# Storing two result tiles of a batched matmul in three transfers each: 112, 8 and 8 partitions over two DMA queues

## The chip, the cores and the metric

The kernel runs on one core of a Trainium2 chip. The metric is device time in microseconds (us), the median of several executions. A core has a matrix engine (TensorE, "PE" in the profile, with its weight loads as "PEld"), VectorE ("DVE"), ScalarE ("ACT"), GpSimd ("POOL") and SyncE ("SP"). They work on an on-chip memory of 128 partitions and on the matrix engine's accumulators. Transfers between this memory and the large outer memory ("dram") run on sixteen DMA engines; an instruction on GpSimd, SyncE or ScalarE issues such a transfer into that engine's own queue, and the transfer tells of its end by a semaphore.

## The reference

```python
def setup_inputs():
    return {
        "a": np.random.randn(1024, 64, 64).astype(np.float32),
        "b": np.random.randn(1024, 64, 64).astype(np.float32),
    }

def reference(a, b):
    return np.matmul(a, b).astype(np.float32)
```

1024 independent products of 64 x 64 matrices. Each of `a`, `b` and the result has 16.8 MB, and each is moved once.

## The kernel before

The batch is cut into 16 tiles `t` of 64 matrices for `b` and the result, and 8 double tiles `s` of 128 matrices for `a`. A tile of `b` or of the result is 1 MB.

**Loads.** `load_a` (L70) brings a double tile in four parts: three by GpSimd's queue, which convert to bf16 on the way (L74), and one by SyncE's queue in fp32 (L78). The first double tile is loaded by SyncE and ScalarE (L91). `load_b` (L94) brings a tile of `b` by SyncE's queue for even `t` and by ScalarE's for odd `t` (L97), three tiles ahead.

**Compute.** Each `a` is transposed, by VectorE (L128) for double tiles 1 to 3 and by the matrix engine (L138, copied out at L141) for the others. `spread` (L146) lays the transposed blocks into a block-diagonal operand (L154, L164), `cast` (L169) turns `b` into bf16: VectorE at L173, and for the last tile ScalarE (L180) and VectorE (L178) by quarters. `multiply` (L187) runs 64 matmuls per tile (L218), and `evacuate` (L200) copies the accumulators into the result tile `o_sb` (L206), mostly on ScalarE; for odd tiles from 7 on, half of the second half's copies go to VectorE.

**Stores.** `o_sb` holds, for each of 128 partitions, eight pieces (`gh`) of 1 KB, 8 KB in all. In the outer memory each such piece is one run of 1 KB:

```python
    o_v = out.rearrange("(t gh x) (mo w) n -> t (x mo) gh (w n)", gh=8, x=8, w=4)
```

`multiply` does not store: it leaves functions in `held[t]`, which `store(t)` (L183) calls later. `HOLD = 2` (L38), so the main loop (L258) calls `store(t - 1)` at the end of its turn for `t` (L286). For tiles 0 to 13 there is one function, which calls `put(0, 8)` (L194): one transfer of all 128 partitions, 1 MB, issued by GpSimd (L195; `store_queue`, L65). Tile 14 goes in two halves by SyncE, tile 15 in quarters by ScalarE and SyncE in turns. Result tiles come from a pool of eight buffers.

**Order.** The program's order is each engine's order: an engine issues its transfers and runs its instructions as written, and waits where an operand isn't ready. SyncE's list from tile 11 on is: the load of `b`'s tile 14, then the stores of tiles 14 and 15. ScalarE issues the load of `b`'s tile 15 in the loop's turn 12. GpSimd's last two instructions are the stores of tiles 12 and 13.

Of the kernel before, what the change touches and what calls it, by code (L numbers as in the profile page):

```python
# [13 lines left out]
def kernel(  # L14
# [14 lines left out]
    nc = tc.nc  # L29
# [7 lines left out]
    N_BD = 2  # L37
    HOLD = 2  # L38
    ON_DVE = (1, 2, 3)

    a_v = a.rearrange("(s g h) (mp v) k -> s h g mp (v k)", h=4, g=32, v=16)
    b_v = b.rearrange("(t g h) (kp u) n -> t (h kp) g (u n)", h=4, g=16, u=2)
    o_v = out.rearrange("(t gh x) (mo w) n -> t (x mo) gh (w n)", gh=8, x=8, w=4)
# [19 lines left out]
    held = {}  # L63

    def store_queue(t, lo):  # L65
        if t < n_t - 2:
            return nc.gpsimd
        return nc.scalar if t == n_t - 1 and lo % 4 == 0 else nc.sync

    def load_a(s):  # L70

        a_sb = a_pool.tile([128, 3, 16, 64], bf16, name="a_sb")
        for h in range(3):
            nc.gpsimd.dma_start(  # L74
                out=a_sb[:, h, :, :].rearrange("p v k -> p (v k)"), in_=a_v[s, h], single_packet=True
            )
        a_raw = a_pool.tile([128, 16, 64], fp32, name="a_raw")
        nc.sync.dma_start(out=a_raw[:].rearrange("p v k -> p (v k)"), in_=a_v[s, 3])  # L78
        a_tiles[s] = a_sb, a_raw
# [53 lines left out]
    def transpose(s, j):  # L133
        a_cols = abf_tiles[s][:].rearrange("p v h k -> p v (h k)").bitcast(fp32)
        for wl in range(2):
            at_ps = t_psum.tile([128, 4, 128], fp32, name="at_ps")
            for vo in range(4):
                nc.tensor.transpose(  # L138
                    at_ps[:, vo, :], a_cols[:, 4 * vo + 2 * j + wl, :], identity[:]
                )  # L140
            nc.scalar.copy(  # L141
                at_tiles[s][:, :, 2 * j + wl, :, :],
                at_ps[:].rearrange("p vo (g mp) -> p g mp vo", mp=4),
            )

    def spread(t):  # L146
        bd = bd_tiles[t % N_BD]
        at_sb = at_tiles[t // 2]
        for h in range(4):
            rows = slice(32 * h, 32 * h + 32)  # L150
            if t // 2 in ON_DVE:
                for i in range(2):
# [34 lines left out]
    def multiply(t):  # L187
        at_bd = bd_tiles[t % N_BD][:].rearrange("p g (j wl) h mp vo -> p j g (wl h mp vo)", j=2)
        at_bd = at_bd.bitcast(bf16).rearrange("p j g (c u) -> p j g c u", u=2)
        b_bf = bbf_tiles.pop(t)  # L190
        last = t == n_t - 1
        o_sb = o_pool.tile([128, 8, 2, 2, 64], fp32, name="o_sb")

        def put(lo, n):  # L194
            store_queue(t, lo).dma_start(  # L195
                out=o_v[t, :, lo : lo + n, :],
                in_=o_sb[:, lo : lo + n].rearrange("p gh j wl n -> p (gh j wl n)"),
            )

        def evacuate(o_ps, gh, n, copies):  # L200

            for par in range(2):
                for wl in range(2):
                    src = o_ps[64 * wl : 64 * wl + 64, :, par, :, :]
                    dst = o_sb[64 * par : 64 * par + 64, gh : gh + n, :, wl, :]
                    copies[2 * par + wl](dst, src)  # L206

        for half in range(2):
            if not last:
                o_ps = o_psum.tile([128, 4, 2, 2, 64], fp32, name="o_ps")  # L210
            for g8 in range(8):
                if last and g8 % 4 == 0:
                    o_ps = t_psum.tile([128, 2, 2, 2, 64], fp32, name="at_ps")
                g = 8 * half + g8
                gl = (g8 % 4 if last else g8) // 2
                for j in range(2):
                    for u in range(2):
                        nc.tensor.matmul(  # L218
                            o_ps[:, gl, g % 2, j, :],
                            at_bd[:, j, g, :, u],  # L220
                            b_bf[:, g, 64 * u : 64 * u + 64],
                            start=(u == 0),
                            stop=(u == 1),
                        )
                if last and g8 % 4 == 3:
                    copy = nc.scalar.copy if g8 == 3 else nc.vector.tensor_copy
                    evacuate(o_ps, g // 4 * 2, 2, [copy] * 4)
            if not last:
                copies = [nc.scalar.copy] * 4
                if half and t % 2 and t > 2 * max(ON_DVE):  # L230
                    copies[2:] = [nc.vector.tensor_copy] * 2
                evacuate(o_ps, 4 * half, 4, copies)
        if last:
            held[t] = [lambda q=q: put(2 * q, 2) for q in range(4)]
        else:
            whole = t < n_t - 2
            held[t] = [lambda q=q: put(q, 8 if whole else 4) for q in ([0] if whole else [0, 4])]

    with tc.manual_schedule():
        load_first_a()  # L240
# [17 lines left out]
        for t in range(n_t):  # L258
            s, half = t // 2, t % 2
            if t + 1 < n_t:  # L260
                spread(t + 1)
                cast(t + 1)
            if t + B_AHEAD < n_t:
                load_b(t + B_AHEAD)
            if half == 0 and 0 < s < n_s - 1 - A_AHEAD:
                load_a(s + 1 + A_AHEAD)
            if half == 0 and 0 < s < n_s - 1 and s + 1 not in ON_DVE:
                transpose(s + 1, 1)
            multiply(t)
            if t == 0:  # L270
                transpose_dve(1, 0)
                transpose_dve(1, 1)
                a_tiles.pop(1)
                load_a(A_AHEAD)
                load_a(A_AHEAD + 1)
            if t and s + 2 in ON_DVE and (half or s):
                for part in [0, 1] if t == 1 else [half]:
                    transpose_dve(s + 2, part)
                if half:
                    a_tiles.pop(s + 2)  # L280
            elif half == 0 and 0 < s and s + 2 < n_s:
                regroup(s + 2)
            elif half == 1 and s + 2 < n_s:
                transpose(s + 2, 0)
            if t >= HOLD - 1:
                store(t - HOLD + 1)  # L286
# [32 lines left out]
```

## Time and profile before

| what | value |
|---|---|
| median of 3 runs | 133.72 us (133.55 to 133.87) |
| the profiled execution | 133.61 us, of which span 131.8 us |
| busy share of the span: PE, PEld, DVE, ACT, POOL | 45%, 43%, 77%, 67%, 24% |
| outer memory read, written | 33.55 MB, 16.78 MB; 382 GB/s over the span |
| stores by GpSimd (L195) | 14 of 1024 KB, median 22.7 us from issue to landing |
| stores by SyncE | 2 of 512 KB (5.5 us), 2 of 256 KB (5.2 us) |
| stores by ScalarE | 2 of 256 KB (4.7 us) |
| issue of the stores of tiles 12 and 13 on GpSimd | at 109.93 us (0.90 us) and 115.72 us (1.35 us) |

The span runs from the first to the last instruction of the program; what lies around it (1.8 us here) is start and end of the execution. "Landing" is the last completion of a transfer. The store of tile 12 takes from 109.93 to 122.9 us to land, that of tile 13 from 115.72 to 125.6 us.

### The profile page before, as it was taken

The page shows a single profiled execution, that of the slowest core. Times are in us where ns is not written, and L with a number is a line of the kernel's source. Part 1 is how long each engine was busy: PE and PEld are TensorE (multiplying, and loading weights), DVE is VectorE, ACT ScalarE, POOL GpSimd, SP SyncE. Part 2 cuts the span into 40 slices and gives each one's busy share as a digit, 9 for nine tenths or more (in the row PEclk, how much of TensorE's full clock was granted, in tenths as well). Part 3 has the DMA queues.
Part 4 walks back from the last instruction along what each step waited for, and adds up shares of the span by engine and source line. Part 5 has one row for each costly group of instructions (what it writes and reads, how often), then busy time and mean ns, then how long its engine had stood idle before and what let it go on. Part 6 is the DMA issues. An engine that isn't in the chain of part 4 may idle for free.

```text
span 131.8 us, 2750 instructions
## 1 busy us (share of the span) xinstructions
PE 59.6 (45%) x1104; PEld 56.7 (43%) x1104; DVE 101.8 (77%) x144; ACT 88.1 (67%) x158; POOL 31.9 (24%) x43
## 2 busy tenths in 40 slices
PE   0006405730550640908662883299369619465000
PEld 0006305730550630908552872298368618464000
DVE  5930399529999984999999998699999997898300
ACT  2125414999495096492999989469969996549920
POOL 8991000340054000618031204300420302040000
PEclk9999975798568555595999599558968975579855
DMA  3999999999999999999999999999999999999993
GB/s 68 372 334 313 306 313 280 280 311 321 327 299 400 362 306 297 393 393 400 321 285 357 403 395 362 308 299 385 395 391 393 390 390 397 399 395 406 390 383 136
DMA packets 19020, 44.99 MB, mean 341 GB/s; under 512 B 1088, under 2 KB 3136, under 8 KB 19008
## 3 DMA queue, kind: packets, MB, share of 16 engines
q0 software_dynamic: 6832, 20.19, 50.6%
q1 hardware_dynamic: 7120, 14.68, 30.7%
q10 hardware_dynamic: 5056, 9.96, 20.1%
q8 instruction: 8, 0.13, 0.4%
q14 instruction: 4, 0.03, 0.1%
HBM read 33.55 MB, written 16.78 MB: 382 GB/s over the span
## 4 chain that ended last, share of the span: by engine, by line
DMA 53%; ACT 15%; DVE 14%; PE 6%; issue 5%; SPq 2%; ACTq 0%; DVEq 0%
DMA b_sb<-in_b_dram 53%; ACT o_sb L206 12%; PE o_ps L218 6%; DVE at_bd L164 4%; DVE b_bf L173 4%; DVE at_bd L154 2%; ACT b_bf L173 1%; DVE at_sb L128 1%; DVE o_sb L206 1%; DVE a_bf L109 1%; SPq L91 1%; ACT a_bf L126 1%; SPq L97 1%; ACT b_bf L180 1%; DVE a_bf L112 0%
## 5 line engine op out<-in xcount | busy, mean ns | idle before, releaser
L206 ACT COPY o_sb<-o_ps 64x512 f32<-64x512 f32 x112 | 65.0, 581 | 17.9 <-PE o_ps L218 13.5
L218 PEld LDWEIGHTS <-at_bd 128*128 128x128 bf16 x1024 | 45.2, 117 | 52.6 <-DVE b_bf L173 40.5
L218 PE MATMUL o_ps<-b_bf,at_bd 128*128 128x64 bf16 x960 | 45.6, 223 | 48.7 <-DVE b_bf L173 35.0
L164 DVE COPY at_bd<-at_sb 32x1024 f32<-32x1024 f32 x40 | 29.6, 739 | 6.6 <-ACT at_sb L141 5.6
L195 POOL DMA_DIRECT2D out_dram<-o_sb x14 | 15.4, 1103 | 46.1 <-ACT at_sb L141 20.6
L154 DVE COPY at_bd<-at_sb 32x512 f32<-32x512 f32 x48 | 22.0, 457 | 1.1
L74 POOL DMA_DIRECT2D a_sb<-in_a_dram x21 | 12.4, 606 | 38.5 <-DVE at_sb L128 33.2
L173 DVE CAST b_bf<-b_sb 128x2048 bf16<-128x2048 f32 x14 | 17.2, 1227 | 5.2 <-DMA b_sb<-in_b_dram 4.9
L138 PE MATMUL at_ps<-identity,a_bf 128*128 128x128 f32 x80 | 12.9, 329 | 11.0 <-ACT a_bf L106 11.0
L138 PEld LDWEIGHTS at_ps<-identity,a_bf 128*128 128x128 f32 x80 | 11.7, 176 | 11.0 <-issue 11.0
L141 ACT COPY at_sb<-at_ps 128x512 f32<-128x512 f32 x20 | 10.8, 591 | 2.7 <-PE at_ps L138 2.0
L128 DVE STREAM_TRANSPOSE at_sb<-a_sb 128x512 f32<-128x512 f32 x9 | 8.9, 1065 | 0.0
L128 DVE STREAM_TRANSPOSE at_sb<-a_bf 128x512 f32<-128x512 f32 x3 | 3.1, 1049 | 4.0 <-ACT a_bf L126 4.0
L206 DVE COPY o_sb<-o_ps 64x512 f32<-64x512 f32 x8 | 5.5, 690 | 0.2
L106 ACT CAST a_bf<-o_sb 128x1024 bf16<-128x1024 f32 x2 | 2.1, 1045 | 5.0 <-DMA o_sb<-in_a_dram 5.0
L173 ACT CAST b_bf<-b_sb 128x2048 bf16<-128x2048 f32 x1 | 1.9, 1897 | 4.0 <-DMA b_sb<-in_b_dram 4.0
L126 ACT CAST a_bf<-a_raw 128x1024 bf16<-128x1024 f32 x3 | 3.1, 1046 | 1.7 <-DMA a_raw<-in_a_dram 1.7
L109 DVE COPY a_bf<-a_sb 128x3072 bf16<-128x3072 bf16 x4 | 4.2, 1045 | 0.0
L106 DVE CAST a_bf<-o_sb 128x1024 bf16<-128x1024 f32 x2 | 2.8, 1383 | 1.8 <-DMA o_sb<-in_a_dram 1.8
L246 DVE MEMSET at_bd<- 128x4096 f32 x1 | 3.5, 3472 | 0.8 <-issue 0.8
L206 DVE COPY o_sb<-at_ps 64x256 f32<-64x256 f32 x8 | 3.4, 422 | 0.5 <-PE at_ps L218 0.4
L180 ACT CAST b_bf<-b_sb 128x512 bf16<-128x512 f32 x2 | 1.1, 616 | 3.5 <-DMA b_sb<-in_b_dram 3.5
(16 smaller groups left out, 15.4 us busy)
## 6 DMA issues: line engine op xcount, KB each, us to landing
out_dram<-o_sb POOLq DMA_DIRECT2D x14, 1024.0 KB, 22.7
a_sb<-in_a_dram POOLq DMA_DIRECT2D x21, 256.0 KB, 15.9
a_raw<-in_a_dram SPq DMA_DIRECT2D x7, 512.0 KB, 17.3
o_sb<-in_a_dram SPq DMA_DIRECT2D x2, 512.0 KB, 5.9
o_sb<-in_a_dram ACTq DMA_DIRECT2D x2, 512.0 KB, 7.0
out_dram<-o_sb SPq DMA_DIRECT2D x2, 512.0 KB, 5.5
out_dram<-o_sb SPq DMA_DIRECT2D x2, 256.0 KB, 5.2
out_dram<-o_sb ACTq DMA_DIRECT2D x2, 256.0 KB, 4.7
```

The lines of the kernel that those rows point to most:

```text
L74: nc.gpsimd.dma_start(out=a_sb[:, h, :, :].rearrange("p v k -> p (v k)"), in_=a_v[s, h], single_packet=True)
L106: copy(a_bf[:, :, h, :], a_sb[h].rearrange("p (v k) -> p v k", v=16))
L109: nc.vector.tensor_copy(a_bf[:, :, 0:3, :], cast_sb[:].rearrange("p h v k -> p v h k"))
L128: nc.vector.transpose(at_tiles[s][:, h].rearrange("p g w mp vo -> p w vo g mp"), pairs.rearrange("p (vo w kp) -> p w vo kp", vo=4, w=4),)
L138: nc.tensor.transpose(at_ps[:, vo, :], a_cols[:, 4 * vo + 2 * j + wl, :], identity[:])
L141: nc.scalar.copy(at_tiles[s][:, :, 2 * j + wl, :, :], at_ps[:].rearrange("p vo (g mp) -> p g mp vo", mp=4),)
L154: nc.vector.tensor_copy(bd[rows, 8 * i : 8 * i + 8, :, h, :, :].rearrange("p g w mp vo -> p (g w) (mp vo)"), at_sb[block : block + 32, h]. ...
L164: nc.vector.tensor_copy(bd[rows, :, :, h, :, :].rearrange("p g w mp vo -> p (g w) (mp vo)"), at_sb[rows, half].rearrange("p g w mp vo -> p ...
L173: (nc.vector.tensor_copy if t else nc.scalar.copy)(b_bf[:], b_sb[:])
L195: store_queue(t, lo).dma_start(out=o_v[t, :, lo : lo + n, :], in_=o_sb[:, lo : lo + n].rearrange("p gh j wl n -> p (gh j wl n)"),)
L206: copies[2 * par + wl](dst, src)
L218: nc.tensor.matmul(o_ps[:, gl, g % 2, j, :], at_bd[:, j, g, :, u], b_bf[:, g, 64 * u : 64 * u + 64], start=(u == 0), stop=(u == 1),)
```

## The change

Tiles 12 and 13 get three store functions instead of one. GpSimd's transfer covers partitions 0 to 111; partitions 112 to 119 and 120 to 127 are two transfers issued by SyncE. All three are called at the same place in the program, where `store(12)` and `store(13)` stood. What is stored, and where, is the same.

```diff
     ON_DVE = (1, 2, 3)
+    CUT = (12, 13)
...
+        def put_rows(lo, hi):
+            (nc.sync if lo else nc.gpsimd).dma_start(
+                out=o_v[t, lo:hi, :, :],
+                in_=o_sb[lo:hi].rearrange("p gh j wl n -> p gh (j wl n)"),
+            )
...
             whole = t < n_t - 2
             held[t] = [lambda q=q: put(q, 8 if whole else 4) for q in ([0] if whole else [0, 4])]
+            if t in CUT:
+                held[t] = [lambda c=c: put_rows(*c) for c in ((0, 112), (112, 120), (120, 128))]
```

## The prediction

> **What bounds the kernel now.** I read, in this order, the chain of work that ended last, the table of DMA queues, the busy time by stretch at the end, SyncE's and GpSimd's rows of the timeline, and then the trace's own records of DMA packets and completions.
>
> The chain of work that ended last begins with this summary, and two of its later pieces (start, length, what) are the ones that matter here:
>
> ```profile
> DMA 53%; ACT 15%; DVE 14%; PE 6%; issue 5%; SPq 2%; ACTq 0%; DVEq 0%
> ```
>
> ```profile
> 102.47 14.73 DMA b_sb<-in_b_dram
> ...
> 117.28 0.06 ACT b_bf L180
> ...
> 125.87 0.37 ACT o_sb L206
> ```
>
> More than half of the chain is transfers of `b`. The last one, tile 15's, is issued at 102.47 and is whole at 117.20; the cast, the matmuls and the evacuations of the last tile then run to 126.24, and the last store is issued at 126.27. The span ends at 131.8, so the last 5.5 us are transfers again. The DMA queues:
>
> ```profile
> q0 software_dynamic: 6832, 20.19, 50.6%
> q1 hardware_dynamic: 7120, 14.68, 30.7%
> q10 hardware_dynamic: 5056, 9.96, 20.1%
> q8 instruction: 8, 0.13, 0.4%
> ```
>
> The shares add up to over 100%: the sixteen DMA engines have work all the time. q0 is GpSimd's queue, q1 SyncE's, q10 ScalarE's. The end by stretches of half a microsecond (last two columns: mean busy share of the sixteen engines, GB/s):
>
> ```profile
> 128.00:128.50 0.50, 0.00 (x0) 0.00 (x0) 0.00 (x0) 0.00 (x0) 0.00 (x0) 0.50 1.11 387
> 128.50:129.00 0.50, 0.00 (x0) 0.00 (x0) 0.00 (x0) 0.00 (x0) 0.00 (x0) 0.50 1.00 350
> 129.00:129.50 0.50, 0.00 (x0) 0.00 (x0) 0.00 (x0) 0.00 (x0) 0.00 (x0) 0.50 0.74 260
> 129.50:130.00 0.50, 0.00 (x0) 0.00 (x0) 0.00 (x0) 0.00 (x0) 0.00 (x0) 0.50 0.58 205
> 130.00:130.50 0.50, 0.00 (x0) 0.00 (x0) 0.00 (x0) 0.00 (x0) 0.00 (x0) 0.50 0.30 102
> ```
>
> No compute engine works, and the transfers thin out in steps: full at 128.5, half of it (0.58 of 1.11) a microsecond and a half later. The sixteen do not finish together. The trace gives every transfer sixteen completions, one per DMA engine. Those of the last store come at 129.1, 129.2, 129.2, 129.3, 129.6, 129.7, 129.9, 130.0, then 130.5 three times, 130.6 three times, 130.8 and 130.9: an early eight and a late eight. The last packets end about 0.33 us before the completions: 128.78 to 129.64 for the early, 130.15 to 130.58 for the late. The same gap is in the completions of tiles 11 to 13. It grows during the run: one straggler from 30 us, two from 48, and so on, each after one of the eight 16 KB packets of queue q8 (29.4, 47.9, 63.5, 71.4, 83.0, 94.4, 103.6, 114.5 us, some 0.96 us each). Each such packet holds up one engine, and eight have been hit. So the end is the work of eight late engines, which never idle.
>
> **The change, part by part.** A result tile is 128 rows (partitions) of 8 KB; each engine carries eight rows of it. Per engine a row costs two 4 KB packets on GpSimd's queue, which start 161 ns apart where nothing else runs: 0.322 us. On SyncE's queue the same row goes as eight 1 KB packets, 42.3 ns apart in the last stores: 0.338 us.
>
> *Removed:* 16 of 128 rows of tiles 12 and 13 from GpSimd's transfer. At seven rows an engine instead of eight, each engine saves 0.322 us per tile, 0.644 us in all.
>
> *Added:* four transfers of 8 rows. No row in this trace shows a transfer of fewer than 128 partitions, so I bound it. A row never appears split over engines here (the sixteen packet sequences of every store come out at whole rows), so eight rows are one row on each of eight engines: +0.338 us per piece there. Both pieces of a tile on the same eight: +0.677 a tile. If these are the early eight, each early engine gains 2 x (0.677 - 0.322) = +0.71 us and each late one loses 0.644. If they are the late eight, it is the other way round. If rows are split evenly over sixteen, a tile costs each engine 2 x 0.169 - 0.322 = +0.016, nothing. The bounds for the late engines are thus -0.64 and +0.71.
>
> Which eight? The records hold no engine number. But packets with equal start times within a queue stand in a fixed order, and on GpSimd's queue between 115 and 125 us I can tell the tied ones apart by phase: in the three early/late pairs that tie, each time anew from tile to tile, the early one's packet is listed first. If the table runs by engine number, the late eight are the later numbers; I take pieces to be dealt from the first engine on, so to the early eight. That is a choice, not a measurement.
>
> [...]
>
> The end, then: late engines 130.58 - 0.64 = 129.94; slowest early engine 129.64 + 0.71 = 130.35, which now ends last. The last packet moves from 130.58 to 130.35, **-0.23 us**.
>
> *Issue and queues.* SyncE has one load left before its stores:
>
> ```profile
> 96.63 0.69 SPq L97 DMA_DIRECT2D b_sb<-in_b_dram  x1
> 120.83 5.36 SPq L195 DMA_DIRECT2D out_dram<-o_sb  x4
> ```
>
> Its queue waits from 97.4 to 120.83. The four issues, at 377 to 1215 ns each by its other stores, fall at about 109 (tile 12's evacuation ends at 108.91) and 115.2 (tile 13's ends at 115.16) and are over by 117.6: hidden, with 3 us to spare. They add two waits on evacuations, and behind them stand only the stores of tiles 14 and 15, which are due later. If the cover were gone, up to 2.4 us would push the first store of tile 14. GpSimd issues as many instructions as before (0.90 and 1.35 us for these two) and nothing follows them. No later tile reuses the buffers of tiles 12 and 13.
>
> *A transfer that overtakes.* Tile 12's rows stood behind earlier stores on q0 and moved only after b's last load was whole. On q1 they move as soon as tile 14's load is through (110.3 to 112.0), taking turns with b's last load. That puts 16 packets x 42.3 ns = 0.68 us in front of it on the eight engines. Fourteen of its completions come at 115.7 to 115.9, one at 116.7 and the last at 117.2, on an engine just hit by the q8 packet at 114.5. Delayed early engines would complete by 116.6, still under 117.2: cast L180 does not move. On the late eight it would move to 117.9, +0.68 us.
>
> [...]
>
> **Sum.** The profiled execution took 133.61 us, 131.8 of it span; 133.61 - 0.23 = 133.38. It lay 0.11 under the median of 133.72, so against the median 133.49; I say **133.5**.
>
> **The rivals.**
> - *The pieces land on the late eight.* The end comes 0.71 us later and so does b's last load by 0.68, which is the same engines' delay, not a second one: 134.4. For it: nothing names the engines. Against: the order of ties. It decides as soon as the last engine of b's last load is among the eight.
> - *No relief: 112 rows go as 14 engines x 8.* The engines that carry the pieces have ten rows a tile: 129.64 + 4 x 0.338 = 130.99, +0.41: 134.1. For it: every transfer seen has eight rows per engine. This also stands for slow reading of the pieces, of about 0.16 us each or more.
> - *Nothing moves:* pieces spread evenly, or what the late gain is lost to the new shapes: +0.03, 133.75. Two spare transfers that don't do what they say.
> - *More relief:* the early engines' spread of 0.86 us is an accident of this execution; if they end together near their mean of 129.17, the late ones decide and all of 0.64 is won: 133.1.
>
> **How the numbers follow.** Forecast 0.42, late eight 0.20, no relief 0.13, nothing 0.15, more relief 0.10. A measurement here tells about 0.2% (0.27 us) from no change: 133.45 to 133.99. The forecast sits at that edge: I put 0.18 of its chance on faster, 0.21 on the same, 0.03 on slower. With the 0.10, faster is 0.28; with 0.12 of "nothing", the same is 0.33; the rest, 0.39, slower. The likeliest case's own range is 133.2 to 133.8; the whole range, from full relief to the late eight, 133.1 to 134.5.
>
> **What would show it.** Right: the last store's completions in one group within a microsecond, the busy share of 129.0 to 130.0 near 1.1 and then falling at once, 256 more 1 KB packets on q1, cast L180 still at 117.3. The late eight: the share falls to half earlier and lasts longer, L180 near 117.9. No relief: some engines skip tile 12 on q0. The prediction is wrong if b's last load lands later, or the gap between the halves stays.

## The result, and the profile after

The changed kernel takes 137.25 us (median of 4 runs, 137.1 to 137.35); before takes 133.8 us beside it (133.55 to 133.94). The ratio is 1.0262 with a 95% interval of 1.0245 to 1.028: **3.45 us slower**, where the prediction said 133.5 and at most 134.5. The profiled execution has a span of 135.2 us against 131.8.

First the compute side. The chain of waits, its summary and three of its pieces (start, length, what):

```profile
DMA 52%; ACT 17%; DVE 16%; issue 4%; PE 3%; SPq 2%; DVEq 0%; ACTq 0%
...
102.38 15.06 DMA b_sb<-in_b_dram
...
117.53 0.07 ACT b_bf L181
...
126.10 0.37 ACT o_sb L213
```

It is nearly the chain of before (the numbers of source lines have moved by one and by seven): the last load of `b` is whole at 117.44 instead of 117.20, the first cast of the last tile starts at 117.53 instead of 117.28, and the last evacuation ends at 126.47 instead of 126.24. A quarter of a microsecond is lost here. The other 3 us must lie after it or beside it, in the transfers. SyncE's rows of the timeline:

```profile
96.54 0.69 SPq L98 DMA_DIRECT2D b_sb<-in_b_dram  x1
108.84 7.11 SPq L202 DMA_DIRECT2D out_dram<-o_sb  x4
121.07 6.92 SPq L196 DMA_DIRECT2D out_dram<-o_sb  x4
```

The four pieces are issued from 108.84 to 115.95, long before SyncE's next store. That row only grows at its end, from 5.36 to 6.92 us. The busy time by stretches (last two columns: busy share of the sixteen DMA engines, GB/s), first before, then the changed kernel:

```profile
120.00:122.00 2.00, 0.38 (x14) 0.26 (x9) 1.93 (x5) 1.95 (x4) 0.00 (x0) 1.00 1.02 406
122.00:124.00 2.00, 0.00 (x0) 0.00 (x0) 0.95 (x3) 1.93 (x6) 0.00 (x0) 1.00 1.00 393
124.00:126.00 2.00, 0.00 (x0) 0.00 (x0) 0.00 (x0) 1.93 (x6) 0.00 (x0) 0.50 1.07 384
126.00:128.00 2.00, 0.00 (x0) 0.00 (x0) 0.00 (x0) 0.24 (x1) 0.00 (x0) 0.50 1.08 382
```

```profile
118.00:120.00 2.00, 1.65 (x32) 1.65 (x33) 1.06 (x3) 1.95 (x5) 0.00 (x0) 0.50 1.03 404
120.00:122.00 2.00, 1.95 (x37) 1.79 (x34) 1.68 (x4) 1.95 (x4) 0.00 (x0) 0.50 1.04 365
122.00:124.00 2.00, 0.00 (x0) 0.00 (x0) 1.69 (x5) 1.94 (x5) 0.00 (x0) 0.50 1.02 307
124.00:126.00 2.00, 0.00 (x0) 0.00 (x0) 0.00 (x0) 1.93 (x6) 0.00 (x0) 0.50 1.00 324
126.00:128.00 2.00, 0.00 (x0) 0.00 (x0) 0.00 (x0) 0.45 (x2) 0.00 (x0) 0.50 1.05 341
128.00:130.00 2.00, 0.00 (x0) 0.00 (x0) 0.00 (x0) 0.00 (x0) 0.00 (x0) 0.50 1.01 351
130.00:132.00 2.00, 0.00 (x0) 0.00 (x0) 0.00 (x0) 0.00 (x0) 0.00 (x0) 0.50 0.50 174
132.00:134.00 2.00, 0.00 (x0) 0.00 (x0) 0.00 (x0) 0.00 (x0) 0.00 (x0) 0.50 0.10 35
```

These are the rows to learn from: from 120 to 128 us the engines are as busy as ever (shares of 1.00 to 1.05), yet they move 307 to 365 GB/s, where the same stretches of before have 382 to 406. Both kernels move the same kinds of packets there, so busy and slow means that packets take longer. The trace has each packet's time. Of GpSimd's 4 KB packets that start after 118 us, 3 of 606 take over 200 ns before and 75 of 575 after, up to 1131 ns, against a usual 165. All the time above 169 ns adds up to 16.2 us of engine time, against 0.4. Shared evenly over sixteen engines that would be 1.0 us. It isn't: the sixteen completions of tile 13's store on GpSimd's queue come from 123.73 to 128.68 us, where before has them from 123.55 to 125.61. The last packet of all ends at 133.79 instead of 130.58, 3.21 us later.

The queues:

```profile
q0 software_dynamic: 6768, 19.93, 49.6%
q1 hardware_dynamic: 7408, 14.94, 30.6%
q10 hardware_dynamic: 5056, 9.96, 19.6%
```

As meant, 0.26 MB went from q0 to q1. The slow packets are on GpSimd's queue while the 112-row transfers move: they start between 119.43 and 127.84 us; the first engine is through with tile 11 at 118.58, the last one with tile 13 at 128.68. They are not in the pieces: SyncE's 1 KB packets between 110 and 121 us, which are the pieces', take 48 ns on average, against 46 in the last stores of before.

### The profile page after: what moved, and what is told of

Same layout as the page of the kernel before. It is cut to its first block, busy times and chain, and to the rows that moved or that the text cites. A ratio compares the mean times of both kernels' runs of the same rounds, so it can differ in the third digit from the quotient of the medians.

```text
span 135.2 us, 2757 instructions
## 1 busy us (share of the span) xinstructions
PE 61.5 (45%) x1104; PEld 58.2 (43%) x1104; DVE 101.4 (75%) x144; ACT 88.0 (65%) x158; POOL 32.4 (24%) x43
## 4 chain that ended last, share of the span: by engine, by line
DMA 52%; ACT 17%; DVE 16%; issue 4%; PE 3%; SPq 2%; DVEq 0%; ACTq 0%
DMA b_sb<-in_b_dram 52%; ACT o_sb L213 13%; DVE at_bd L165 6%; PE o_ps L225 3%; DVE b_bf L174 3%; DVE at_bd L155 2%; DVE a_bf L110 2%; ACT b_bf L174 1%; DVE at_sb L129 1%; DVE o_sb L213 1%; SPq L92 1%; DVE a_bf L113 1%; ACT a_bf L127 1%; ACT at_sb L142 1%; SPq L98 1%
## 5 line engine op out<-in xcount | busy, mean ns | idle before, releaser
L225 PEld LDWEIGHTS <-at_bd 128*128 128x128 bf16 x1024 | 45.9, 118 | 52.2 <-DVE b_bf L174 40.2
L225 PE MATMUL o_ps<-b_bf,at_bd 128*128 128x64 bf16 x960 | 44.9, 221 | 48.1 <-DVE b_bf L174 37.9
L196 POOL DMA_DIRECT2D out_dram<-o_sb x12 | 13.8, 1146 | 36.0 <-ACT at_sb L142 13.6
L139 PE MATMUL at_ps<-identity,a_bf 128*128 128x128 f32 x80 | 13.7, 344 | 11.4 <-ACT a_bf L107 11.4
L139 PEld LDWEIGHTS at_ps<-identity,a_bf 128*128 128x128 f32 x80 | 12.6, 185 | 11.4 <-issue 11.4
L202 POOL DMA_DIRECT2D out_dram<-o_sb x2 | 2.1, 1048 | 9.4 <-issue 5.2
```

Source lines behind the costliest of these rows:

```text
L139: nc.tensor.transpose(at_ps[:, vo, :], a_cols[:, 4 * vo + 2 * j + wl, :], identity[:])
L196: store_queue(t, lo).dma_start(out=o_v[t, :, lo : lo + n, :], in_=o_sb[:, lo : lo + n].rearrange("p gh j wl n -> p (gh j wl n)"),)
L225: nc.tensor.matmul(o_ps[:, gl, g % 2, j, :], at_bd[:, j, g, :, u], b_bf[:, g, 64 * u : 64 * u + 64], start=(u == 0), stop=(u == 1),)
```

## The experiments

The changes are shown against the changed kernel unless said otherwise. "A" is the theory that the 112-row transfer is the cost, "B" that the 8-row pieces are.

**One piece of 16 rows.**

```diff
- ... for c in ((0, 112), (112, 120), (120, 128))
+ ... for c in ((0, 112), (112, 128))
```

> Tiles 12 and 13 as 112 rows by GpSimd and one transfer of 16 rows by SyncE, in place of two of 8. Theory A (the 112-row transfer is the cost: its rows reach the DMA engines in another pattern than 128 rows do, and engines slow each other while reading): still slow, +2.5 to +3.5 us against before, 4 KB packets of GpSimd's queue over 200 ns on average between 121 and 128 us, as in the changed kernel. Theory B (the 8-row pieces are the cost, by loading only eight engines): the 16 rows go evenly over sixteen engines, so the time returns to before, within 0.3 us.

Measured: 136.36 us, ratio 1.0201 (1.0159 to 1.0243). Still 2.8 us slower; 66 of 562 packets of 4 KB over 200 ns, and 212 ns on average between 121 and 128 us, as theory A had it. The 112 rows are most of the cost. The interval just misses that of the changed kernel (1.0245 to 1.028), so the two 8-row pieces may cost some 0.7 us more than one of 16; the two were measured beside different runs of before, and no run separates this further.

**The same bytes, cut by columns.**

```diff
- ... put_rows, c in ((0, 112), (112, 120), (120, 128))
+ ... put_part, c in ((0, 128, 0, 7), (0, 128, 7, 1))   # rows lo, hi; pieces of 1 KB from g on, n of them
```

> Tiles 12 and 13 cut the other way: all 128 rows by GpSimd with 7 of their 8 KB, the last 1 KB of all 128 rows by SyncE. As many bytes change queue as in the changed kernel, but every transfer has 128 rows. Theory A: within 0.3 us of before, packets of GpSimd's queue at 165 ns. Theory C (moving an eighth of the stores to SyncE's queue, ahead of the last load of b, is the cost): +1 us or more. Theory B expects no change either.

Measured: 133.94 us, ratio 1.0028 (1.0013 to 1.0044). Two packets of 564 over 200 ns. As many bytes on SyncE's queue cost 0.4 us, a little more than theory A's 0.3, and not 3.45. Moving them is not the cause; theory C falls.

**Sixteen pieces of 8 rows.**

```diff
+ parts = [(0, 128, 0, 7)] + [(8 * i, 8 * i + 8, 7, 1) for i in range(16)]
```

> As the split by 7 KB and 1 KB, but the last 1 KB of the 128 rows goes as sixteen transfers of 8 rows on SyncE's queue: sixteen pieces a tile that load eight engines only, and no 112-row transfer. It shifts the same 0.64 us off the late engines and onto the early ones as the prediction wanted. Theory A: no slower than before, between -0.6 and +0.3 us. Theory B: slower by as much as the changed kernel or more, +3 us, since there are eight times as many pieces; a little of that may come from 32 issues on SyncE (0.3 us each, 9.6 us, before 120.8 us).

Measured: 139.48 us, ratio 1.0438 (1.0405 to 1.047). Slower than theory A allowed. SyncE's timeline, then two stretches:

```profile
107.64 22.20 SPq L202 DMA_DIRECT2D out_dram<-o_sb  x32
129.97 3.34 SPq L196 DMA_DIRECT2D out_dram<-o_sb  x4
```

```profile
124.00:126.00 2.00, 0.00 (x0) 0.00 (x0) 0.00 (x0) 1.93 (x6) 0.00 (x0) 0.50 0.14 36
126.00:128.00 2.00, 0.00 (x0) 0.00 (x0) 0.00 (x0) 0.14 (x1) 0.00 (x0) 0.50 0.56 176
```

The 32 issues take until 129.84: they wait 7.1 us in all for `b`'s last two loads to land and 0.5 us for earlier pieces, and some of them last 1.1 us. The stores of tiles 14 and 15 stand behind them: issued at 129.97 instead of 120.83. The DMA engines idle (a share of 0.14). This is a queue's order, not slow transfers, and the run decides nothing between A and B; only 2 of its 540 packets of 4 KB are over 200 ns.

**Two transfers of 64 rows.**

```diff
- ... for c in ((0, 112), (112, 120), (120, 128))
+ ... for c in ((0, 64), (64, 128))          # both by nc.gpsimd
```

> Tiles 12 and 13 as two transfers of 64 rows, both by GpSimd: nothing goes to SyncE, every engine gets 4 + 4 rows as before, the packets are the same 4 KB. [...] Theory B and a theory of uneven row counts (7 and 9 instead of 8): no change, within 0.3 us.

Measured: 136.87 us, ratio 1.023 (1.0187 to 1.0273), 44 of 595 packets over 200 ns. No piece, no second queue, by the expectation four plus four rows for each engine, and 3.3 us slower. So neither the pieces nor uneven row counts are needed for a loss of this size.

**Other places in the outer memory.**

```diff
- out=o_v[t, lo:hi, :, :],
+ out=flat_v[t, lo:hi, :, :],     # rows of 8 KB one after the other
```

> As the changed kernel (112, 8 and 8 rows), but the rows of tiles 12 and 13 are written one after the other, 8 KB each, in place of eight runs of 1 KB that lie 128 KB apart; the results of these two tiles stand in other places of the output. Theory A in the form 'the engines hinder each other on the on-chip side, where they read': still slow, +2.5 to +3.8 us, with long packets on GpSimd's queue. Theory D (they hinder each other in the outer memory, by the places that seven rows in turn write): back to before, within 0.5 us.

Measured: ratio 1.0233 (1.0185 to 1.0281), some 3.1 us slower. Other places are written and the loss stays; theory D falls.

**Sixteen pieces, of tile 11 alone.**

> Tile 11 alone: all 128 rows by GpSimd with 7 KB each, the last 1 KB of the rows as sixteen transfers of 8 rows by SyncE, issued from 103 us on, so that their waits for one another end before SyncE's stores at 120.8. No 112-row transfer. It moves 8 KB off each late engine and onto each early one. If the sixteen-piece run of tiles 12 and 13 was slow by its issue waits and not by the pieces' transfers: -0.5 to +0.2 us against before, no idle stretch of the DMA engines. Theory B (pieces are slow to move): +1 us or more.

Measured: 134.26 us, ratio 1.0022 (1.0005 to 1.0039), 0.3 us slower, just above the +0.2 that was expected. SyncE's issues still reach to 123.24 and push its first store to 123.34; most of their waiting, 12.0 us, is for `b`'s loads and not for one another. Pieces of 8 rows alone do not cost microseconds, but they bring nothing either.

**One tile at a time.**

```diff
- CUT = (12, 13)
+ CUT = (12,)        # and, in the next run, (13,)
```

> Only tile 12 is cut in 112, 8 and 8 rows. Theory A, cost by tile: +1 to +2 us, together with the run that cuts tile 13 alone the +3.45 us of both. If the cost comes from the two tiles' transfers meeting each other, each alone costs under 0.8 us.

> Only tile 13 is cut in 112, 8 and 8 rows. Theory A, cost by tile: +1 to +2.5 us, more than tile 12 since less of it runs beside the last load of b. If the cost comes from the two tiles' transfers meeting each other: under 0.8 us.

Measured: 135.83 us, ratio 1.0156 (1.0109 to 1.0202), and 136.48 us, ratio 1.0191 (1.0166 to 1.0216). Each tile costs by itself, 1.9 and 2.6 us, with 39 and 33 packets over 200 ns. The sum, 4.5, is more than the 3.45 of both; that what is lost on one engine partly hides what is lost on another would explain it, and was not tested.

The run with tile 12 alone also parts the 112 rows from the pieces in time. The pieces' last packet ends at 116.18 us; the long packets start between 119.40 and 125.67. So pieces under way are not what the 112-row transfer meets.

**The cut in the middle of the run.**

```diff
- CUT = (12, 13)
+ CUT = (4, 5)
```

> The same three transfers for tiles 4 and 5 in place of 12 and 13, in the middle of the run, where loads of a and b go on beside the stores. Theory A with its condition (engines hinder each other only while several read the result tiles at once; here they spend about half of their time on loads, which write): long packets rare, +0.0 to +1.0 us. If the price belongs to the 112-row transfer as such, wherever it runs, and is kept to the end because the engines never idle: +2.5 to +3.5 us.

Measured: 137.2 us, ratio 1.0269 (1.0237 to 1.0301). By the time alone the second expectation holds, but the profile says something else. The 112-row transfers of tiles 4 and 5 move until 93.4 us. First the changed cut, then before:

```profile
70.00:80.00 10.00, 8.41 (x144) 8.29 (x144) 9.73 (x13) 9.29 (x18) 2.18 (x2) 0.66 1.04 393
80.00:90.00 10.00, 5.14 (x80) 4.91 (x80) 6.98 (x9) 7.00 (x13) 1.08 (x2) 0.83 1.08 321
```

```profile
70.00:80.00 10.00, 7.45 (x144) 7.03 (x144) 9.74 (x13) 9.27 (x19) 1.45 (x2) 0.83 1.03 394
80.00:90.00 10.00, 5.20 (x78) 5.08 (x75) 8.18 (x11) 6.93 (x13) 1.88 (x2) 0.66 1.07 322
```

The engines move as much as before, and of GpSimd's 781 packets of 4 KB from 72 to 94 us one takes over 200 ns. So the first expectation holds for the packets: beside loads the 112 rows show no price in the rate here. (From 104 us on 58 packets of 128-row stores take over 200 ns, most of them under 250; no run explains these.) The time is lost on SyncE's queue. Its timeline, first with the cut, then before:

```profile
60.09 6.97 SPq L202 DMA_DIRECT2D out_dram<-o_sb  x2
67.16 0.54 SPq L79 DMA_DIRECT2D a_raw<-in_a_dram  x1
```

```profile
61.55 5.17 SPq L78 DMA_DIRECT2D a_raw<-in_a_dram  x1
```

The load of `a` behind the pieces is issued to the end at 67.70 instead of 66.72, 1.0 us later. More is lost in what follows: of the sixteen completions of `b`'s load issued at 71.03, eight come from 86.42 to 88.69 us and the other eight from 94.36 to 96.15, where before has all sixteen from 86.49 to 88.86. That fits pieces that stand ahead of it on the eight engines which carry them. A later load of `b` goes out at 103.36 instead of 96.63, and from 120 to 124 us the DMA engines' busy share is 0.56.

**112 rows on SyncE's queue, and its control.** Tiles 12 and 13 as before; tile 14 by SyncE.

```diff
+ CUT = (14,)        # all by nc.sync
+ ... for c in ((0, 112), (112, 128))       # control: ((0, 128),)
```

> Tiles 12 and 13 as before; tile 14, which SyncE stores in two halves, goes as 112 rows and 16 rows, both by SyncE. Theory A (the pattern of rows, whichever queue): slower than the next run by +1 to +2.5 us, with 1 KB packets well over 46 ns at the end. Theory E (only GpSimd's queue handles 112 rows badly): within 0.4 us of the next run.

> Control for the run with tile 14 as 112 and 16 rows: tile 14 as one transfer of 128 rows by SyncE, issued after both halves are evacuated, 2.4 us later than the first half was. Both theories: within 0.5 us of before, since the DMA engines have the stores of tiles 12 and 13 to do until 124 us.

Measured: 135.74 us, ratio 1.0155 (1.0129 to 1.0182), and for the control 133.67 us, ratio 1.0012 (0.9995 to 1.0029). First the 112 rows, then the control:

```profile
126.00:128.00 2.00, 0.00 (x0) 0.00 (x0) 0.00 (x0) 0.00 (x0) 0.00 (x0) 0.50 1.03 285
128.00:130.00 2.00, 0.00 (x0) 0.00 (x0) 0.00 (x0) 0.00 (x0) 0.00 (x0) 0.50 0.99 293
```

```profile
126.00:128.00 2.00, 0.00 (x0) 0.00 (x0) 0.00 (x0) 0.00 (x0) 0.00 (x0) 0.50 1.07 367
128.00:130.00 2.00, 0.00 (x0) 0.00 (x0) 0.00 (x0) 0.00 (x0) 0.00 (x0) 0.50 1.02 347
```

The same sign on the other queue: 2.1 us more than the control, full share, fewer GB/s, and now the 1 KB packets are long (208 of 2048 over 60 ns, 39 in the control). Theory E does not fit. The 16 rows were not run without the 112, so their own part in the 2.1 us is open.

**Only the on-chip rows differ.** Two GpSimd transfers of 64 rows to the same places of the output as in the 64 and 64 run; what is read changes.

```diff
+ def put_from(lo, src):
+     nc.gpsimd.dma_start(out=o_v[t, lo : lo + 64, :, :],
+                         in_=o_sb[src : src + 64].rearrange(...))
+ ... put_from(*c) for c in ((0, 32), (64, 32))      # next run: ((0, 0), (64, 0))
```

> Tiles 12 and 13 as two GpSimd transfers of 64 rows each, as in the run with 64 and 64 rows, to the same places of the output, but both read on-chip rows 32 to 95 (these tiles' results are then in part others' rows). Bytes, row counts, packets, queue and outer places are those of that run; only the on-chip rows differ. [...] If it is any transfer with other than 128 rows: +2.5 to +3.5 us.

> [...] If the on-chip rows decide: slower than the run with 64 and 64 rows, +4 to +7 us, packets near 330 ns. If any transfer with other than 128 rows costs the same: +2.5 to +3.5 us, no different from the run before it.

Measured: rows 32 to 95, 133.47 us, ratio 1.0002 (0.999 to 1.0013); rows 0 to 63, 138.68 us, ratio 1.0387 (1.0367 to 1.0407). Rows 32 to 95 first:

```profile
122.00:124.00 2.00, 0.00 (x0) 0.00 (x0) 1.15 (x3) 1.93 (x5) 0.00 (x0) 1.00 1.01 395
124.00:126.00 2.00, 0.00 (x0) 0.00 (x0) 0.00 (x0) 1.46 (x4) 0.00 (x0) 0.76 1.07 382
```

and rows 0 to 63:

```profile
122.00:124.00 2.00, 0.00 (x0) 0.00 (x0) 0.48 (x2) 1.94 (x5) 0.00 (x0) 0.84 0.99 195
124.00:126.00 2.00, 0.00 (x0) 0.00 (x0) 0.00 (x0) 1.83 (x5) 0.00 (x0) 0.50 1.01 196
126.00:128.00 2.00, 0.00 (x0) 0.00 (x0) 0.00 (x0) 0.00 (x0) 0.00 (x0) 0.50 0.96 232
```

5.2 us lie between two kernels that differ in one number, the first on-chip row. With rows 32 to 95 nothing is lost (3 of 591 packets over 200 ns, as in before), and a 64-row transfer is as good as one of 128. With rows 0 to 63 the engines are fully busy at half the rate (195 against 395 GB/s), and packets cluster between 300 and 360 ns, twice 165. For transfers of 64 rows this settles that **the on-chip rows which are read decide the rate: from 122 to 124 us 395 GB/s with rows 32 to 95 and 195 with rows 0 to 63, at shares of 1.01 and 0.99.** That engines which read rows 0 to 63 hold each other up is a reading; it fits packets of twice the usual time, but which rows meet was not shown, and the expectation's 330 ns and +4 to +7 us were the author's estimate. For 112 rows it is inferred that the rows are the cause: the signs are the same (long packets, a full share, fewer GB/s), and the pieces, the queue and the places written are excluded, but no run took 112 rows from another first row.

**The balance alone.** Tile 12, all rows with 7 KB by GpSimd, the last 1 KB in four transfers.

```diff
+ cuts = (0, 49, 98, 126, 128)
+ parts = [(0, 128, 0, 7)] + [(lo, hi, 7, 1) for lo, hi in zip(cuts, cuts[1:])]
```

> Tile 12 alone: all 128 rows by GpSimd with 7 KB each, and the last 1 KB of the rows by SyncE in four transfers of 49, 49, 28 and 2 rows. If few engines carry a transfer whose row count has few divisors up to 16 (7 engines for 49 rows), some 8 KB move from the late engines to the early ones, as the prediction wanted, with few rows read off their usual engine. The prediction's balance alone: -0.35 to -0.1 us against before. If the balance is worth nothing, or these four transfers hinder the others while reading: 0.0 to +0.6 us.

Measured: 133.89 us, ratio 1.0028 (1.0017 to 1.0038). No gain; the last packet ends at 130.60, as before. The first 49 rows have eight completions, one at once and seven with the data, read here as seven engines. The last store's completions come from 129.28 to 130.29 for the first eight and from 130.30 to 130.96 for the others (before: 129.14 to 129.96 and 130.49 to 130.91): the early half ends 0.1 to 0.4 us later, about as much as executions differ, and the late half does not end earlier. No version here beats before.

## Why the prediction was wrong

**The step that failed** is in the part on what is removed: "At seven rows an engine instead of eight, each engine saves 0.322 us per tile, 0.644 us in all." It took the packet time of a 128-row transfer, 161 ns from start to start, for a transfer of 112. Sixteen times seven fits as a count: in the run with one piece of 16 rows, seven of the eight later completions move by 2.2 to 2.4 us from tile 11 to tile 12 (compared in order of time), which is fourteen packets of 161 ns, where before they move by 2.6. But the packets did not keep their 161 ns. Instead of taking 0.32 us less per engine, the 112-row transfers held some engines up by microseconds: packets up to 1131 ns, 16.2 us of engine time in all, tile 13's last completion 3.07 us later, the last packet of the kernel 3.21 us later. The cause that the runs point to is that the shorter transfer puts engines on other on-chip rows than a 128-row transfer does; that the rows decide the rate is shown for 64 rows (395 against 195 GB/s) and inferred for 112. As the late engines stay busy to the end, nothing of it was won back.

**What bounds the kernel** was read rightly: the sixteen engines, up to the last packet. So a loss on them appears in the time: the last packet ends 3.21 us later, and the kernel takes 3.45 us more.

**The rivals.** "No relief" named slow reading, but in the pieces and at 0.16 us each, and priced at +0.41. The bounds, -0.64 and +0.71 us, were drawn for the four added transfers, since no row showed a transfer of fewer than 128 partitions, and not for the shortened one, which no row showed either. This is the lesson of the miss: a transfer whose shape changes is a new transfer, even where it only gets smaller.

**The rows that are read.** Slow reading was weighed for the 8-row pieces alone, whose packets stayed at 48 ns. The runs put most of the cost in the large transfer (2.8 us with one piece of 16 rows beside it), and the last pair of 64-row transfers has 395 and 195 GB/s by the on-chip rows alone. Which rows each engine carries in a transfer of 112, and which of them meet, no run here shows; nor does one show why a few engines pay for the long packets, so that 16.2 us make 3.2 and not 1.0.

**Eight engines a piece** held: the trace has nine completions for each 8-row piece in place of sixteen, for tile 12's first one at 109.3 and eight from 114.9 to 116.6. The one near the issue and the eight with the data are read here as eight engines that carry a piece. Whether these were the early eight was not tested.

**The overtaking piece**: the prediction had 0 or 0.68 us for the first cast of the last tile; it came 0.25 us later. The load behind it was issued 0.09 us earlier and took 15.06 us instead of 14.73.

**Issue on SyncE** was hidden as reckoned: 277 to 346 ns an issue, over by 115.95. The middle-of-the-run and sixteen-piece runs show what this cover is worth: where SyncE has work behind the pieces, half of a load's completions came up to 7.3 us later than before, and the last stores went out 9.1 us later.

**The gain of 0.23 us** from evening out the halves was not found in the two runs that tried to even out the halves without the 112 rows: ratios of 1.0022 (sixteen pieces of tile 11) and 1.0028 (the balance alone). The run cut by columns, which moves nothing between the halves, has 1.0028 too, so part of that may be small costs of more transfers, and the size of the balance term stays open.

## What to carry to other kernels

Cut a transfer by its columns rather than by its partitions: all 128 rows with 7 of 8 KB cost 0.4 us here where 112 rows cost 2.8. If part of the rows must go, try the rows that are then read (two transfers of 64 rows moved 395 GB/s from rows 32 to 95 and 195 from rows 0 to 63), and, where the packets are of the same kind, look behind a full busy share with falling GB/s for long packets (here 307 GB/s at a share of 1.02, and 75 of 575 packets over 200 ns). (Before has 322 GB/s at a share of 1.07 from 80 to 90 us with no such trouble: GpSimd's queue loads `a` there in 2 KB packets of some 172 ns.) The place counts too: with the same cut 75 of 575 packets took over 200 ns where stores alone ran, and 1 of 781 where loads ran beside them. Before a transfer moves to another queue, list what stands behind it there until its data is ready.

## What the runs showed of the hardware that was not expected

- Two transfers of 64 rows, 0 to 63 and 64 to 127, lost 3.3 us, and two of rows 0 to 63 lost 5.2. No run reads rows 64 to 127 in both. If those are as slow as rows 0 to 63, a reading fits the difference, as an estimate of the author's: the late engines run some 1.2 us behind (tile 13's completions in before come at 124.08 and 125.30 on average), about one 64-row transfer (four rows of 0.322 us, 1.3 us), so that much of the time one half of the engines reads the low rows while the other reads the high ones. This was not tried by itself.
- With only tile 12 cut, the stretches from 124 to 130 us have 340 to 363 GB/s at shares of 0.99 to 1.05, though the stores there are of 128 rows. Before has 384 and 382 from 124 to 128 at shares of 1.07 and 1.08, and the 1 KB packets take 46 ns there against 48, so more than half of the difference goes with the share; why the share is lower stays open.
- The 8-row pieces on SyncE's queue set apart the eight engines that carry them: with the cut in the middle of the run, a load behind them has eight completions in time and eight some 7 us late, where before has all sixteen within 2.4 us.
